# Aligning the operand tiles of the wide matmuls modulo 512 bytes in a bidirectional GLA and RWKV-7 block

## The chip, the core and the metric

The kernel runs on one core of one Trainium2 chip. The metric is device time: microseconds (us) of one execution, as the median of several. A profile of one execution shows every instruction of the five engines: PE (TensorE, whose weight loads are listed apart as PEld), DVE (VectorE), ACT (ScalarE), POOL (GpSimd) and SP, which issues the DMAs.

## What is computed

One encoder block on 2048 tokens of width 1024, in float32:

```
h  = RMSNorm(x)
p  = h @ W_in                              # columns: GLA | RWKV-7 | merge gates
yA = GLA branch, forward + backward        # chunked gated linear attention
yB = RWKV-7 branch, forward + backward     # delta-rule scans
x  = x + (sigmoid(gA) * yA + sigmoid(gB) * yB) @ W_out
u  = conv3(RMSNorm(x) @ ffn_up)            # 2 x 2752 columns, depthwise conv of width 3
x  = x + (silu(u_gate) * u_val) @ ffn_down
out = RMSNorm(x)
```

## The kernel before

**Wide matmuls.** Each float32 operand of a large product is split into a high part (a cast to float32r) and a low part (the rest), and a product is three passes: high by high, high by low, low by high. A matmul loads a stationary tile of 128 x 128 (a weight load, PEld) and streams a moving tile of 128 x 512 past it into one PSUM bank. Nearly all weights pass through two pairs of buffers, `whi` and `wlo`, in the pool `wp`; a tile of a float32 buffer is 512 bytes per partition for a stationary slice and 2048 for a moving one, so every slice of a buffer begins at the same remainder modulo 512 bytes as the buffer does.

**Stages, in order of time.** To 150 us: first norm, transposes, and the value product (`wvh`, `wvl` moving against `hhi`, `hlo`), all in `mm3` (L240). To 1050: the input projection, 116 units of 24 matmuls (L240, `in_tile`: `whi`/`wlo` stationary, `hhi`/`hlo` moving), with the GLA branch and the operands of RWKV-7 woven in as a side thread; it begins with 64 matmuls of the low-rank gate (L402), whose stationary slice has 64 columns. To about 1970: the RWKV-7 chunk recurrence, 32 steps in an order written out by hand, in which a generator `fill` (L1204) places 8 groups of 4 wide matmuls per step between the dependent small ones; these 1248 matmuls are left-over gate tiles and the GLA output projection. To 2100: the RWKV-7 output projection and merge (384 matmuls at L240). To 2310: output projection (768 matmuls at L240, `woh`/`wol` moving against `whi`/`wlo`) and second norm. To 3170: the up projection in two sweeps over 21 pairs of feature tiles (L1494), seven products of 12 matmuls a pair. Two of the seven, with B11 and B21, take `whi`/`wlo` as stationary; five take `s1` to `s4` from the pool `fw`, made by POOL and DVE one pair ahead. The odd 43rd tile adds 96 matmuls with `whi`/`wlo`. To the end: the down projection, 2016 matmuls (L1705 to L1707, `whi`/`wlo` stationary, `wdh`/`wdl` moving), 64 more at L1709 and L1710, and the last norm.

**What sets places and order.** Pools are stacks: left-side pools grow from the low end of SBUF, one after another, and right-side ones (`wp`, `ev`, `op_`, `opx`) from the high end, so a tile's address follows from the sizes of what was opened before it. `const` (the identity `ident`, the table `vec`, `eps_ln`) is the first left pool and stays open to the end. Outside the recurrence a scheduler orders the instructions; a tile on an address that another tile held waits for that tile's last user.

Of the kernel before, what the change touches and what calls it, by code (L numbers as in the profile page):

```python
# [8 lines left out]
F32 = mybir.dt.float32  # L9
# [3 lines left out]
BF16 = mybir.dt.bfloat16  # L13
# [8 lines left out]
T = 2048  # L22
# [144 lines left out]
def _body(tc, A, out, dump=None, upto=99):  # L167
    nc = tc.nc
    L = _vec_layout()
    sync = nc.sync  # L170
    base = ExitStack()

    def pool(stack, name, bufs=1, space=None, **kw):
        if space is None:
            return stack.enter_context(tc.tile_pool(name=name, bufs=bufs, **kw))
        return stack.enter_context(tc.tile_pool(name=name, bufs=bufs, space=space, **kw))
# [22 lines left out]
    d_act = scratch("d_act", [NAT, 128, T])  # L199
    d_mat = scratch("d_mat", [8, 128, 4, BT])  # L200

    const = pool(base, "const")

    def cload(name, shape, dt=F32, key=None):
        t = const.tile(shape, dt, name=name)
# [8 lines left out]
        o = L[name][0] + i  # L214
        return vec[rows, o:o + 1]

    eps_ln = const.tile([128, 1], F32, name="eps_ln")
    nc.gpsimd.memset(eps_ln, 1e-30)

    s_wp = ExitStack()  # L220
    wp = pool(s_wp, "wp", side="right")
    ev = pool(s_wp, "ev", bufs=3, side="right")
# [52 lines left out]
            nc.vector.tensor_tensor(out=ol, in0=pt, in1=oh.bitcast(F32), op=ALU.subtract)  # L275

    FB, MB = (3, 2, 1), 34
# [1 line left out]
    class Halves:  # L279
        def __init__(self, tiles):  # L280
            self.t = tiles
# [7 lines left out]
    s_hb = ExitStack()  # L289
# [4 lines left out]
    s_h = ExitStack()  # L294
# [12 lines left out]
    s_pg = ExitStack()  # L307
# [80 lines left out]
                sync.dma_start(out=dst[:, b * BT:(b + 1) * BT], in_=o)  # L388
            yield

    # GLA low-rank gate inputs: rows = [hi(32) | lo(32)]
    raw = wp.tile([128, 1024], F32, name="wraw", tag="wraw", bufs=1)
    rv = raw[:, 0:256].rearrange("p (a b) -> p a b", a=8)
    sync.dma_start(out=rv, in_=A["waf"])
# [9 lines left out]
        nc.scalar.copy(out=o[0:64, :], in_=ps[0:64, :])  # L404
        sync.dma_start(out=d_af[:, b * BT:(b + 1) * BT], in_=o[0:64, :])

# [1 line left out]
    s1 = ExitStack()  # L408
    s2 = ExitStack()
    gp = pool(s1, "gp", reuse_waits="tile")  # L410
# [5 lines left out]
    nc.gpsimd.memset(g4[64:128, :, 127:128], 0.0)  # L416
    glow = gp.tile([128, 128], U32, name="glow")
    sync.dma_start(out=glow, in_=A["c_glow"])
    gdiag = gp.tile([128, 128], F32, name="gdiag")
    sync.dma_start(out=gdiag, in_=A["c_gdiag"])  # L420
    wa2 = gp.tile([64, 4, 128], F32, name="wa2")
    sync.dma_start(out=wa2, in_=A["wa2"])
    dec = gp.tile([128, 4, 16], F32, name="dec")
# [222 lines left out]
        pl = nc.scalar.preload_act_table_set(LNEXP)  # L646
    act_tail = [pl]

# [1 line left out]
    R = {}  # L650

    def rwkv_open():
# [69 lines left out]
    def rwkv_prep(p, b):  # L722
# [26 lines left out]
            last = nc.scalar.preload_act_table_set(LNEXP)  # L749
        act_tail[0] = last  # L750
        yield
        # normalised key direction
        tmp = R["rp"].tile([128, 512], F32, name="tmp", tag="tmp")
        kk = R["rp"].tile([128, 512], F32, name="kkt", tag="kkt")
        nc.scalar.activation(out=tmp, in_=sk, func=AF.Square, scale=vc("kk", p))
# [54 lines left out]
    def prep():  # L810
        while done[0] < 10:
            yield
        for b in range(NB):
            act_tail[0] = rwkv_shared(b)
            yield
        for p in range(4):
            while done[0] < 13 + 3 * p:
                yield
            for b in range(NB):
                yield from rwkv_prep(p, b)  # L820
# [10 lines left out]
    if upto < 3:  # L831
        return finish(locals())

# [1 line left out]
    s3 = ExitStack()  # L835
    cp = pool(s3, "cp", reuse_waits="tile")
    cl = pool(s3, "cl", reuse_waits="tile")
# [498 lines left out]
    if upto < 4:  # L1336
        return finish(locals())

# [1 line left out]
    s5 = ExitStack()  # L1340
    op_ = pool(s5, "op", side="right", reuse_waits="tile")
    woh = op_.tile([128, KT, D], F32R, name="woh")
# [3 lines left out]
    s_pg = ExitStack()  # L1346
    pg = pool(s_pg, "pg2", bufs=3, space=PSUM)
    s4 = ExitStack()
# [57 lines left out]
    if upto < 5:  # L1406
        return finish(locals())

# [1 line left out]
    s_h2 = ExitStack()  # L1410
    h2a = pool(s_h2, "h2a", reuse_waits="tile")
    h2p = pool(s_h2, "h2p", reuse_waits="tile")
# [7 lines left out]
    s_t = ExitStack()  # L1420
    s_pg = ExitStack()
# [97 lines left out]
    s_pg.close()  # L1519
    s5.close()  # L1520

# [1 line left out]
    # u = W^T h2 by Winograd's form of the 2 x 2 block product: feature tiles (gate, value) x halves of k x blocks of tokens  # L1523
    h2q = pool(s_h2, "h2q", reuse_waits="tile")
    mat(h2q, "T4")
    s6 = ExitStack()
# [49 lines left out]
        nbank[0] += 1  # L1576
        return pus[(nbank[0] - 1) % 8 >= 3].tile([128, 512], F32, name="pu", tag="pu")

    # columns of u: sweep 0 [2 unused | block 1 | block 2], sweep 1 [0 | block 0 | 2 of block 1 | 2 of block 2 | block 3 | 0]
    COLS = ((slice(2, 514), slice(514, 1026)), (slice(1, 513), slice(517, 1029)))  # L1580
    SEG = (((3, 511, 513), (514, 511, 1024)), ((1, 513, 0), (516, 513, 1535)))

# [91 lines left out]
    if upto < 7:  # L1674
        return finish(locals())

# [1 line left out]
    s7 = ExitStack()  # L1678
    fd = pool(s7, "fd", reuse_waits="tile")
    wd0 = pool(s7, "wd0", reuse_waits="tile")  # L1680
    wda = pool(s7, "wda", reuse_waits="tile")
    pd = pool(s7, "pd", space=PSUM)
# [109 lines left out]
def finish(l):  # L1792
    if l["dump"] is not None:
        for n, o in l["dump"].items():
            l["nc"].sync.dma_start(out=o, in_=l[n][0:o.shape[0]])
    for n in ("s5", "s4", "s3", "s_hb", "s_t", "s_pg", "s_h2", "s_h", "s_wp", "base"):
        if n in l:
            l[n].close()

# [18 lines left out]
```

## Time and profile before

| what | value |
|---|---|
| median of 3 executions | 3684.48 us (3683.09 to 3687.15) |
| span of the profiled execution, first to last instruction | 3676.5 us |
| PE busy, matmuls | 3428.3 us (93%) x21208 |
| PE busy, weight loads | 2685.7 us (73%) |
| DVE, ACT, POOL busy | 2402.8 (65%), 1478.6 (40%), 1301.9 us (35%) |
| mean granted TensorE clock | 0.958 |

The profiled execution's span is 8.0 us under the median; the difference lies ahead of the first instruction and behind the last. Matmuls are pipelined: the next one starts while the last one drains, so what a stream of them costs is read from the distance of their starts and not from the busy time of one.

### The profile page before, as it was taken

The numbers are of one execution on the slowest core, as the hardware profiler recorded it, in microseconds if no ns is written. First come the engines' busy times: TensorE is split into PE (matmuls) and PEld (weight loads), VectorE is DVE, ScalarE is ACT, GpSimd is POOL, SyncE is SP. The second block draws the span as 40 slices with busy tenths as digits, with TensorE's granted clock in tenths as the row PEclk, the third lists the DMA queues.
The fourth block names the chain that finished last, engine by engine and source line by source line (L and its number), as shares of the span: only waits on it lengthen the run. The fifth ranks groups of instructions, "written<-read, shape, count | busy, mean of one in ns | idle before, by whom it ended". The sixth has DMA issues, their size and how long they took to land.

```text
span 3676.5 us, 56674 instructions
## 1 busy us (share of the span) xinstructions
PE 3428.3 (93%) x21208; PEld 2685.7 (73%) x21208; DVE 2402.8 (65%) x3926; ACT 1478.6 (40%) x2678; POOL 1301.9 (35%) x1105
## 2 busy tenths in 40 slices
PE   7999999999979899888887899999989999999999
PEld 6787778766667677766665788877768777777777
DVE  5207764687846766766788476889898989723222
ACT  4214443555544444454545333434344344411111
POOL 1122221234442343333325411666676666100000
PEclk9999999999988889998898999999989999999999
DMA  4233444688882655566789846322232222523221
GB/s 152 85 115 108 135 133 134 197 219 230 229 252 92 186 171 163 163 196 184 222 237 307 312 149 192 119 80 78 78 129 91 79 81 81 172 76 113 82 80 62
DMA packets 408338, 547.98 MB, mean 149 GB/s; under 512 B 62528, under 2 KB 251584, under 8 KB 408064
## 3 DMA queue, kind: packets, MB, share of 16 engines
q1 hardware_dynamic: 408064, 544.36, 48.3%
q8 instruction: 167, 2.74, 0.3%
q14 instruction: 107, 0.88, 0.1%
HBM read 361.79 MB, written 181.93 MB: 148 GB/s over the span
## 4 chain that ended last, share of the span: by engine, by line
PE 53%; DVE 21%; DMA 9%; issue 8%; ACT 4%; POOL 3%; SPq 1%; DVEq 0%; ACTq 0%; POOLq 0%
PE pg L240 20%; PE pu L1494 6%; PE pd L1705 4%; PE pd L1706 4%; PE pd L1707 4%; PE pf L1204 4%; DVE cv L1599 2%; DVE tm L915 2%; DVE XX L916 2%; DVE cv L1600 2%; DVE ug L1499 1%; DVE uv L1499 1%; DVE s1l L226 1%; PE psc L867 1%; DMA wraw<-win 1%
## 5 line engine op out<-in xcount | busy, mean ns | idle before, releaser
L876 POOL TENSOR_TENSOR Lt<-Lt,mk 64x512 f32<-64x512 f32 x128 | 148.9, 1163 | 471.4 <-ACT Lt L875 462.5
L1554 POOL TENSOR_TENSOR rw<-rw 128x512 f32<-128x512 f32 x168 | 274.6, 1654 | 4.4 <-DMA rw<-wup 1.0
L1705 PE MATMUL pd<-wdh,whi 128*128 128x512 f32 x672 | 265.4, 397 | 0.9 <-DVE ug L1499 0.9
L1706 PE MATMUL pd<-wdl,whi 128*128 128x512 f32 x672 | 265.2, 395 | 0.0
L1707 PE MATMUL pd<-wdh,wlo 128*128 128x512 f32 x672 | 263.1, 395 | 0.0
L240 PE MATMUL pg<-hhi,whi 128*128 128x512 f32 x928 | 253.5, 408 | 3.7 <-ACT whi L225 3.7
L240 PE MATMUL pg<-hlo,whi 128*128 128x512 f32 x928 | 256.4, 409 | 0.0
L240 PE MATMUL pg<-hhi,wlo 128*128 128x512 f32 x928 | 251.9, 406 | 0.0
L226 POOL TENSOR_TENSOR wlo<-wraw,whi 128x1024 fp32r<-128x1024 f32 x46 | 115.3, 2506 | 349.6 <-PE pg L240 171.8
L240 PEld LDWEIGHTS pg<-hhi,whi 128*128 128x128 f32 x928 | 176.7, 193 | 58.4 <-issue 14.8
L240 PEld LDWEIGHTS pg<-hlo,whi 128*128 128x128 f32 x928 | 176.1, 193 | 56.5 <-issue 18.2
L240 PEld LDWEIGHTS pg<-hhi,wlo 128*128 128x128 f32 x928 | 176.6, 193 | 53.8 <-issue 14.7
L1204 PE MATMUL pf<-fop,whi 128*128 128x512 f32 x576 | 178.6, 446 | 20.3 <-ACT whi L225 13.1
L1598 ACT ACTIVATE cv<-ug,vec 128x511 f32<-128x511 f32 (+1 forms) x88 | 72.1, 819 | 248.7 <-DVE ug L1499 248.7
L225 ACT CAST whi<-wraw 128x1024 fp32r<-128x1024 f32 x114 | 119.7, 1050 | 116.9 <-PE pg L240 52.2
L1204 PEld LDWEIGHTS pf<-fop,whi 128*128 128x128 f32 x576 | 113.4, 208 | 51.7 <-ACT whi L225 15.9
L1705 PEld LDWEIGHTS pd<-wdh,whi 128*128 128x128 f32 x672 | 126.4, 188 | 33.6 <-issue 4.3
L1599 DVE SCALAR_TENSOR_TENSOR cv<-ug,vec,cv 128x511 f32<-128x511 f32 (+1 forms) x88 | 125.3, 1424 | 36.0 <-ACT cv L1598 36.0
L1707 PEld LDWEIGHTS pd<-wdh,wlo 128*128 128x128 f32 x672 | 126.4, 188 | 29.9
L1706 PEld LDWEIGHTS pd<-wdl,whi 128*128 128x128 f32 x672 | 126.5, 188 | 29.4
L1694 ACT CAST whi<-wraw 128x1024 fp32r<-128x1024 f32 (+1 forms) x36 | 35.3, 981 | 275.4 <-PE pd L1706 193.1
L1697 DVE TENSOR_TENSOR wlo<-wraw,whi 128x1024 fp32r<-128x1024 f32 (+1 forms) x36 | 39.3, 1092 | 157.9 <-ACT whi L1694 157.9
(469 smaller groups left out, 8645.9 us busy)
## 6 DMA issues: line engine op xcount, KB each, us to landing
rw<-wup SPq DMA_DIRECT2D x84, 512.0 KB, 3.4
wraw<-win SPq DMA_DIRECT2D x74, 512.0 KB, 4.1
Lt<-d_lt SPq DMA_DIRECT2D x64, 512.0 KB, 6.1
d_lt<-arbk SPq DMA_DIRECT2D x96, 256.0 KB, 3.9
d_gate<-ev SPq DMA_DIRECT2D x64, 256.0 KB, 4.0
X<-d_vt SPq DMA_DIRECT2D x64, 256.0 KB, 4.5
U<-d_vt SPq DMA_DIRECT2D x64, 256.0 KB, 7.5
bj<-d_lt SPq DMA_DIRECT2D x128, 128.0 KB, 4.0
```

Of the source, the lines that this page charges most:

```text
L225: (hi_eng or nc.scalar.copy)(out=hi, in_=src)
L226: (lo_eng or nc.vector).tensor_tensor(out=lo, in0=src, in1=hi.bitcast(F32), op=ALU.subtract)
L240: nc.tensor.matmul(ps, (wh, wh, wl)[ph], (xh, xl, xh)[ph], start=(ph == 0 and i == 0), stop=(ph == 2 and i == n - 1))
L876: nc.gpsimd.tensor_tensor(out=Lt[rk_, e], in0=Lt[rk_, e], in1=mb_[rk_], op=ALU.mult)
L915: nc.vector.tensor_tensor(out=o, in0=X[:, 0:j, j:j + 1].to_broadcast([128, j, w]), in1=X[:, j:j + 1, j + 1:32].to_broadcast([128, j, w]), ...
L1204: nc.tensor.matmul(ps, (wh, wh, wl)[ph][:, k0 + k, :], (hi, lo, hi)[ph][:, k, :], start=i == first[u] and k == 0, stop=i == last[u] and k ...
L1494: nc.tensor.matmul(ps, w_, x_, start=i == 0, stop=i == len(mm) - 1)
L1554: ps_ = lambda o, x, y, op: nc.gpsimd.tensor_tensor(out=o, in0=x, in1=y, op=op)
L1599: nc.vector.scalar_tensor_tensor(out=c, in0=u[:, c0 - 1:c0 - 1 + n], scalar=vc("cw0", m), in1=c, op0=ALU.mult, op1=ALU.add)
L1705: nc.tensor.matmul(ps, a, wdh[k][:, cs], start=(k == 0), stop=False)
L1706: nc.tensor.matmul(ps, a, wdl[k][:, cs], start=False, stop=False)
L1707: nc.tensor.matmul(ps, l, wdh[k][:, cs], start=False, stop=False)
```

## The change

It moves tiles to other addresses. Five edits do it:

- `eps_ln` takes 97 columns where one is used. All left pools behind `const` move up by 384 bytes.
- `gdiag` (ones, with twos on the diagonal) becomes bfloat16: it is loaded into a buffer of `ev`, cast by DVE, and takes 256 bytes less, which shifts the rest of the pool `gp`.
- `const` gets a stack of its own, which is closed ahead of the down projection. The pools of that stage then begin where `const` began.
- A tile `fpad` of 24 columns, which nobody reads, stands first in the pool `fd`.
- Comments are removed, so lines of the new file lie up to five lower or higher.

```diff
-    const = pool(base, "const")
+    s_const = ExitStack()
+    const = pool(s_const, "const")
...
-    eps_ln = const.tile([128, 1], F32, name="eps_ln")
+    eps_ln = const.tile([128, 97], F32, name="eps_ln")[:, 0:1]
...
-    gdiag = gp.tile([128, 128], F32, name="gdiag")
-    sync.dma_start(out=gdiag, in_=A["c_gdiag"])
+    gdiag = gp.tile([128, 128], BF16, name="gdiag")
+    gdf = ev.tile([128, 512], F32, name="ev", tag="ev")[:, 0:128]
+    sync.dma_start(out=gdf, in_=A["c_gdiag"])
+    nc.vector.tensor_copy(out=gdiag, in_=gdf)
...
+    s_const.close()
     s7 = ExitStack()
     fd = pool(s7, "fd", reuse_waits="tile")
+    fd.tile([128, 24], F32, name="fpad")
```

In the two built programs the tiles of the wide matmuls begin at these remainders modulo 512 bytes (moving tile, stationary tile, and their difference):

| matmuls | count | before | after |
|---|---|---|---|
| input projection, L240 | 2784 | 96, 480: 128 | 480, 480: 0 |
| low-rank gate, L402 | 64 | 96, 480: 128 | 480, 480: 0 |
| fill of the recurrence, L1204 | 1248 | 96, 480: 128 | 480, 480: 0 |
| merge, L240 | 384 | 96, 480: 128 | 480, 480: 0 |
| up projection with `whi`/`wlo`, L1494 | 1104 | 96, 480: 128 | 480, 480: 0 |
| down projection, L1705 to L1710 | 2080 | 352, 480: 384 | 480, 480: 0 |
| value product, L240 | 384 | 96, 96: 0 | 480, 480: 0 |
| output projection, L240 | 768 | 480, 480: 0 | 480, 480: 0 |
| up projection with `s1` to `s4`, L1494 | 2520 | 96, 96: 0 | 480, 480: 0 |
| gate product of RWKV-7, L708 | 48 | 384, 96: 288 | 256, 480: 288 |

The small float32 matmuls keep their differences, but for transposes against `ident`, which stays at 128.

The order of the instructions on PE, ACT and POOL is the same in both programs, and so is DVE's but for the added cast. SP issues two loads at another place. At the start of the GLA branch (`wa_1301` and `wa_1303` are the tile `wa2`), SP before:

```order
L418 DMA glow<-c_glow 128x128
L420 DMA gdiag<-c_gdiag 128x128
L330 DMA d_vg<-ev 128x512
L405 DMA d_af<-ev 64x512
L422 DMA wa_1301<-wa 64x512
L480 DMA v<-d_vg 128x4x128
L473 DMA af<-d_af 64x512
L405 DMA d_af<-ev 64x512 x3
L230 DMA wraw<-win 128x1024
```

The same place on SP now:

```order
L419 DMA glow<-c_glow 128x128
L425 DMA wa_1303<-wa 64x512
L331 DMA d_vg<-ev 128x512
L406 DMA d_af<-ev 64x512
L483 DMA v<-d_vg 128x4x128
L476 DMA af<-d_af 64x512
L406 DMA d_af<-ev 64x512 x2
L422 DMA ev<-c_gdiag 128x128
L406 DMA d_af<-ev 64x512
L231 DMA wraw<-win 128x1024
```

The load of `gdiag` has moved behind two stores of `d_af`, since its `ev` buffer was the source of one of them. On SP at the passage from the up to the down projection, before:

```order
L1688 DMA wraw<-wdn 128x1024
L1609 DMA d_act<-cv 128x513 x2
L1756 DMA gf<-gn 128x1024
L1688 DMA wraw<-wdn 128x1024
L1753 DMA ev<-d_act 128x512
```

And the load of `gf` (the gain of the last norm) now:

```order
L1618 DMA cv<-cv 64x513
L1621 DMA d_act<-cv 64x513
L1622 DMA d_act<-cv 64x513
L1618 DMA cv<-cv 64x513
L1761 DMA gf<-gn 128x1024
L1758 DMA ev<-d_act 128x512
```

`gf` now lies on the addresses of `ident` and `vec`; its load has moved behind the last convolution, the last reader of `vec`, and ahead of a load of activations.

## Rows read from the trace of the kernel before

**Rows 1.** Busy us of PE, PEld, DVE, ACT, POOL by stretch; PEclk, DMA, GB/s.

```profile
150.00:732.00 582.00, 576.34 (x2776) 450.81 (x2774) 290.19 (x662) 218.63 (x464) 143.94 (x107) 0.99 0.42 134
732.00:1050.00 318.00, 290.58 (x1072) 200.50 (x1073) 258.47 (x332) 179.78 (x270) 136.65 (x98) 0.92 0.84 222
1050.00:1600.00 550.00, 482.19 (x5719) 379.71 (x5719) 348.31 (x561) 259.52 (x564) 205.92 (x213) 0.90 0.57 169
1600.00:2100.00 500.00, 420.81 (x4469) 326.92 (x4468) 352.54 (x607) 236.02 (x489) 204.80 (x184) 0.89 0.82 253
2310.00:2720.00 410.00, 397.73 (x1714) 320.59 (x1713) 372.30 (x383) 166.42 (x227) 284.33 (x208) 1.00 0.24 83
2800.00:3170.00 370.00, 361.68 (x1557) 291.00 (x1555) 334.00 (x359) 154.69 (x208) 220.25 (x208) 1.00 0.25 86
3170.00:3677.00 507.00, 496.91 (x2082) 390.12 (x2080) 161.33 (x368) 91.54 (x144) 0.00 (x0) 0.99 0.30 95
```

**Rows 2.** The same view, L240 alone (PE, PEld), first two stretches.

```profile
150.00:732.00 582.00, 463.06 (x1886) 351.26 (x1884) 0.99 0.42 134
732.00:1050.00 318.00, 229.44 (x832) 163.77 (x833) 0.92 0.84 222
```

**Rows 3.** The chain by line, in the first six of those stretches.

```profile
by line: PE pg L240 68.4%; PE paf L525 2.8%; PE z L488 2.7%; PE po L564 2.6%; PE po L565 2.5%; PE pkv L541 2.3%; PE pn L708 1.7%; PE pkt L527 1.6%; PE pot L583 1.6%; DMA twal<-d_twal 1.3%; PE pab L526 1.1%; DMA pl<-d_rw 1.0%; PE pw L738 1.0
by line: PE pg L240 16.6%; issue 8.9%; DMA d_lt<-arbk 8.6%; DMA wraw<-win 6.3%; DMA twal<-d_twal 5.9%; PE pw L738 4.7%; DVE arbk L785 4.6%; DMA pl<-d_rw 3.0%; DVE sr L690 2.7%; SPq L788 2.4%; DVE cx L771 2.1%; SPq L808 2.0%; POOL arbk L784 
by line: PE pf L1204 17.3%; DVE XX L916 9.0%; DVE tm L915 8.8%; PE psc L867 6.0%; issue 5.6%; DVE TT L927 4.4%; DVE Q L874 4.1%; DMA wraw<-win 3.9%; DVE wlo L226 3.6%; PE py L1016 3.1%; PE py L1018 2.8%; DMA ev<-d_h 2.6%; DVE X L1009 2.3%; 
by line: PE pf L1204 11.0%; issue 6.3%; DMA gt<-d_gate 5.9%; DMA d_m<-ev 4.6%; PE pg L240 4.3%; DMA ev<-d_gate 3.3%; DVE tm L915 3.2%; DVE XX L916 3.0%; DMA Lt<-d_y 2.8%; PE py L1016 2.5%; PE py L1018 2.4%; DVE TT L927 2.2%; PE psc L867 1.7
by line: PE pu L1494 40.7%; issue 20.1%; DVE cv L1599 8.2%; POOL rw L1554 7.6%; DVE ug L1499 3.6%; DVE uv L1499 3.6%; POOL s3l L226 3.4%; ACT cv L1598 3.2%; POOL halo L1594 2.4%; DVE cv L1600 1.5%; DVE s1l L226 1.4%; DVE cv L1608 1.0%; POOL
by line: issue 22.6%; DVE cv L1600 11.4%; DVE s1l L226 10.4%; DVE ug L1499 9.7%; DVE uv L1499 9.1%; DVE cv L1608 8.1%; ACT cv L1598 7.2%; DVE cv L1599 6.9%; PE pu L1494 6.5%; DVE s4l L226 4.5%; POOL s3l L226 2.3%; ACT s3h L225 0.8%; DVE wdl
```

**Rows 4.** Longest pieces of that chain, output projection: start us, us, what.

```profile
2219.17 14.30 PE pg L240 x63
2242.71 14.30 PE pg L240 x63
```

**Rows 5.** The chain's longest piece in the input projection.

```profile
149.91 131.53 PE pg L240 x566
```

**Rows 6.** PE by time, up projection: start, us, work [idle before <-releaser].

```profile
2461.00 1.07 PE L1494 MATMUL pu<-mT1h,s1h 128*128 128x512 f32 x4
...
2463.73 1.10 PE L1494 MATMUL pu<-mB21h,whi 128*128 128x512 f32 x4
...
2466.52 1.09 PE L1494 MATMUL pu<-mT4h,s3h 128*128 128x512 f32 x4
...
2480.26 1.21 PE L1494 MATMUL pu<-mT3h,s3l 128*128 128x512 f32 x4 [0.74 <-POOL s3l L226]
```

**Rows 7.** PE in order of time, down projection; 53 matmuls left out.

```profile
3329.88 0.39 PE L1705 MATMUL pd<-wdh,whi 128*128 128x512 f32 x1
...
3342.43 0.40 PE L1705 MATMUL pd<-wdh,whi 128*128 128x512 f32 x1
```

**Rows 8.** PE in order of time at the gate product of L708.

```profile
646.50 1.55 PE L708 MATMUL pn<-gh,g 128*128 128x512 f32 x6
647.89 0.86 PE L240 MATMUL pg<-hhi,wlo 128*128 128x512 f32 x3
```

**Rows 9.** PE in order of time, chunk recurrence.

```profile
1622.63 1.20 PE L1204 MATMUL pf<-fop,wlo 128*128 128x512 f32 x4 [2.31 <-DVE wlo L226]
...
1641.12 2.07 PE L1204 MATMUL pf<-fop,wlo 128*128 128x512 f32 x4
```

**Rows 10.** Group of L531: busy us, mean ns | idle before, what ended it.

```profile
L531 POOL TENSOR_TENSOR comb<-comb,gdiag 128x512 f32<-128x512 f32 x16 | 22.4, 1402 | 24.0 <-DVE comb L530 19.8 <-DVE gnr L249 2.6 <-DVE gnt L251 1.0
```

More of the change, by code (lines that the diff above doesn't have):

```diff
@@ L1795, in finish @@
             l["nc"].sync.dma_start(out=o, in_=l[n][0:o.shape[0]])
-    for n in ("s5", "s4", "s3", "s_hb", "s_t", "s_pg", "s_h2", "s_h", "s_wp", "base"):
+    for n in ("s5", "s4", "s3", "s_hb", "s_t", "s_pg", "s_h2", "s_h", "s_wp", "s_const", "base"):
         if n in l:
```

## The prediction

> **What bounds the kernel now.** I read first the busy times by stretch, where a row is a stretch from:to, its length, and then the busy microseconds of PE, PEld, DVE, ACT and POOL [rows 1]. The reader is to see how much of each stretch PE leaves free: 6 of 582 us in the first part of the input projection, 10 of 507 in the down projection, but 27 of 318, 68 of 550 and 79 of 500 between 732 and 2100, and 12 of 410 and 8 of 370 in the two sweeps of the up projection, where DVE is busy for 91% (372 of 410) and 90% (334 of 370). Then the chain of waits by line, one row for each of the first six stretches [rows 3]: to 732 us it runs through L240 for 68.4% and through other PE lines for nearly all the rest; after that PE's wide matmuls hold 16.6%, 17.3%, and 11.0% plus 4.3%, and the rest is small PE work, DVE, and DMA; in the first sweep of the up projection they hold 40.7%, in the second 6.5%.
>
> Last I read what one wide matmul costs, as the distance of starts, since busy times overlap. In the output projection, where moving and stationary tile begin at the same remainder modulo 512 bytes, 63 matmuls take 14.30 us: **227.0 ns** each [rows 4]. In the input projection, where the remainders differ by 128, 566 in an unbroken piece take 131.53 us: **232.4 ns** [rows 5]. In the down projection, with a difference of 384, the starts of two matmuls that are 54 apart lie 12.55 us apart: 232.4 ns [rows 7]. The up projection has both kinds side by side within one pair: 12 matmuls with `s1` (difference 0) from 2461.00 to 2463.73 take 227.5 ns each, the next 12 with `whi` and `wlo` (difference 128) from 2463.73 to 2466.52 take 232.5 [rows 6]. So I take 5.4 ns as the price of an unequal pair of remainders, and 5.0 in the up projection.
>
> Is it the remainder, and not something else that goes with it? Nearly every unequal wide pair has a partner in `wp` at the high end of SBUF. But the output projection takes the same `whi` against `woh`, and is fast; and the RWKV-7 gate product at L708, whose operands both lie in one pool with a difference of 288, is slow: 6 matmuls from 646.50 to 647.89, 231.7 ns each [rows 8]. Neither the stage nor the distance sorts these four cases; the difference of remainders does.
>
> **The change part by part.** It makes the difference 0 for 7,664 wide matmuls; the order on PE, ACT and POOL stays. At 5.4 ns (5.0 for the 1104 of the up projection) all of them are worth 41 us, if each stood on the path at the full clock. Stage by stage:
>
> - Input projection to 732 us: 1886 matmuls [rows 2] x 5.4 ns = 10.2 us. PE is busy for 99% of the stretch and holds the chain, so all of it counts. About 40 of L240 and the 64 narrower ones of L402 before 150 us add 0.3.
> - Input projection from 732 to 1050 us: 832 matmuls [rows 2], 4.5 us at most. The chain gives L240 16.6% of 318 us = 53 us, 227 matmuls: 1.2 us. The rest hides behind DMAs and DVE, which were late anyway.
> - Fill of the recurrence: 1248 matmuls. The chain gives them 17.3% of 550 and 11.0% of 500 us = 150 us, some 645 matmuls, 3.5 us; with a granted clock of 0.90 and 0.89 [rows 1] a fifth of this time runs at the lower level, where no row shows the price, so I count 0.8 of it: 2.8 us. Bounds: 0 (the next step waits for DVE, as at 1622.63 for 2.31 us [rows 9]) and 5.7.
> - Merge: 384 matmuls, 2.1 us at most; the chain's 4.3% of 500 us is 92 matmuls: 0.5 us.
> - Up projection, first sweep: once a pair PE waits for POOL's split of `s3l` (0.74 us at 2480.26 [rows 6]). POOL reaches that split behind work that waits for the last product of the pair before, so the loop runs from the wait through S1, A12, A22 and S4 to POOL and back. The 12 matmuls with A12 lie in it, the 12 with A11 beside it: they only lengthen the wait. 20 pairs x 12 x 5.0 = 1.2 us (bounds 0 and 2.4).
> - Second sweep: the chain leaves PE 6.5% of 370 us, 24 us, about 105 matmuls, of which two in seven are of the changed kind: 0.15 us (bounds 0 and 2.4). DVE and ACT set this loop. The odd tile and the passage between the sweeps add 0.4.
> - Down projection: 2016 x 5.4 = 10.9 us. PE is busy for 497 of 507 us, POOL for none and DVE for a third [rows 1]; I count 98%: 10.7.
>
> Sum: 10.2 + 0.3 + 1.2 + 2.8 + 0.5 + 1.2 + 0.55 + 10.7 = 27.4 us. With all upper ends it is 39, with input and down projection alone 21.
>
> What it adds: one cast on DVE, for which the first GLA gate waits, and a DMA behind two stores of SP; DVE is busy for half of that stretch (290 of 582 us) and PE has projection matmuls to go on with, so I cost it at 0; if that cover were gone, a DMA and a cast would cost a few microseconds once. POOL's 16 products with `gdiag` (1402 ns each [rows 10]) read a bfloat16 operand now; even half as long again would be 11 us on an engine that is busy for a quarter of the stretch. `gf`, the gain of the last norm, is loaded later, yet long before its first use behind all of the first four row tiles, and its wait is for a convolution that SP's next entries need as well: 0. Whether ACT, DVE or POOL mind the shift of their tiles by 384 bytes no row shows; they touch tiles at remainders of every kind now, and I count nothing.
>
> **A rule against it.** The traces show 227.0 against 232.4 ns [rows 4, 5]. The Trainium skill, SBUF — State Buffer, Who interferes with whom, gives PE two independent read ports, one for the moving operand and one for weight loads, and says that PE and ACT never wait on anyone; TensorE: Matmul & The Clock Gate, Step-by-step: what each phase is for, adds that a weight load takes no read bandwidth from the running matmul. By that rule the place of the two tiles could not matter, the sum would be 0 and the time 3684; the rows of this kernel speak against it, so it stays a rival with a small chance.
>
> **The rivals.** (a) *Everything passes through.* If the idle time between 732 and 3170 us shrinks with PE, since small PE work on the chain starts earlier too, the gain nears 39 us: 3646. For it: PE is in order, and each fill matmul stands ahead of a dependent one. Against it: the waits for DVE, POOL and DMAs in [rows 3, 6, 9]. (b) *Less passes.* Input and down projection alone at the 5.0 ns of the up projection, with something of it lost in the waits behind the first: 19 us, or down to 15: 3667. (c) *The remainder is not the cause*, and the slow pairs stay at 232 ns: 3684. Against it are the four cases above; for it, that no row shows a partner in `wp` against a low pool with equal remainders. (d) *Slower, by the clock.* In the recurrence PE waits for DVE (2.31 us at 1622.63), and some 20 us later the same four matmuls are busy for 2.07 instead of 1.20 us [rows 9]: the clock has gone to its lower level, 1.2 instead of 2.4 GHz. The granted 0.90 and 0.89 mean that some 215 of 1050 us run there. If shorter fill makes PE wait longer, more time may. A microsecond at the lower level costs at most half a microsecond, so the loss passes the gain and 0.2% (7.4 us) from 70 us of it on, when the mean clock of the recurrence falls from 0.895 to 0.86; at 0.85 it would give about 3704. Against it: the fill of a step, 32 matmuls, shrinks by only 0.17 us.
>
> **How the numbers follow.** The profiled span is 3676.5 us, the median 3684.5; the 8.0 us outside the span do not change. Forecast: 3684.5 - 27.4 = **3657 us** (gain 22 to 33 us), chance 0.52. (a) 0.17, (b) 0.18, (c) 0.08, (d) 0.05. A measurement of this kernel can tell about 0.2% (7.4 us) from no change. Faster by more than that: forecast, (a) and (b), 0.87; within it: (c), 0.08; slower: 0.05. For 8 times in 10 the range takes in (a) and most of (b): **3643 to 3669 us**; its lower end is (a) with a little less time at the lower clock.
>
> **What would show it.** In the changed kernel's profile: streams of L240, L1204 and the down projection at 227 ns from start to start, as the output projection has now, with L708 still at 232; the down projection's stretch shorter by about 11 us and the input projection's first part by 10; more idle time of PE ahead of `s3l` in the first sweep, by about 0.06 us a pair; a second sweep of the same length; the recurrence shorter by 2 to 4 us at the same granted clock. It would be wrong if the streams stay at 232 ns (then the remainder is not the cause), if they fall and the stretches don't (then PE was not the bound there), or if the granted clock between 732 and 2100 us moves by more than 0.02.

## The result, and the profile after

The changed kernel takes **3661.02 us** (median, 3651.24 to 3662.31) against 3683.78 us for the kernel before on the same chip: ratio 0.9931, 95% interval 0.9914 to 0.9947. On another chip it took 3661.65 against 3678.61 us, ratio 0.9951 (0.9936 to 0.9965). The gain is 17 to 25 us. The forecast was 3657 us, in a range of 3643 to 3669; the time fell inside it, in its upper half.

The busy times by stretch of the changed kernel (columns as in [rows 1]; its down projection begins some 6 us earlier, so the last stretch is shifted):

```profile
150.00:732.00 582.00, 576.75 (x2804) 456.41 (x2803) 293.35 (x671) 221.19 (x469) 141.63 (x107) 0.99 0.42 136
732.00:1050.00 318.00, 285.33 (x1086) 199.70 (x1084) 258.57 (x328) 178.81 (x269) 143.50 (x103) 0.95 0.81 225
1050.00:1600.00 550.00, 479.90 (x5787) 380.60 (x5788) 348.25 (x560) 262.00 (x573) 198.70 (x209) 0.90 0.57 169
1600.00:2100.00 500.00, 421.73 (x4394) 328.20 (x4392) 352.53 (x607) 232.48 (x482) 205.20 (x184) 0.87 0.81 250
2310.00:2720.00 410.00, 392.02 (x1691) 315.43 (x1689) 371.59 (x384) 166.96 (x227) 283.66 (x208) 1.00 0.24 83
2800.00:3170.00 370.00, 358.47 (x1559) 291.04 (x1558) 333.57 (x359) 153.06 (x206) 216.33 (x207) 1.00 0.26 87
3163.00:3658.00 495.00, 485.00 (x2084) 389.42 (x2082) 161.81 (x369) 91.46 (x144) 0.00 (x0) 0.99 0.31 99
```

PE is as full as before in the first and the last stretch, and the down projection now fits into 495 us instead of 507. In the first sweep of the up projection PE is busy for 392.02 us instead of 397.73, with DVE unchanged. Part of that is the window alone: the changed kernel is 8 us ahead here, and 23 matmuls fewer fall into the stretch. What a pair takes is read below.

PE in order of time, changed kernel: the input projection in an unbroken stream and behind small matmuls, the gate product whose difference stayed at 288, one pair of the up projection, the down projection.

```profile
149.99 1.98 PE L241 MATMUL pg<-hlo,whi 128*128 128x512 f32 x8
...
179.00 1.98 PE L241 MATMUL pg<-hhi,wlo 128*128 128x512 f32 x8
...
307.12 2.01 PE L241 MATMUL pg<-hlo,whi 128*128 128x512 f32 x8
308.98 1.98 PE L241 MATMUL pg<-hhi,wlo 128*128 128x512 f32 x8
310.79 1.98 PE L241 MATMUL pg<-hhi,whi 128*128 128x512 f32 x8
312.60 1.07 PE L241 MATMUL pg<-hlo,whi 128*128 128x512 f32 x4
...
643.00 1.56 PE L711 MATMUL pn<-gh,g 128*128 128x512 f32 x6
644.40 0.85 PE L241 MATMUL pg<-hhi,wlo 128*128 128x512 f32 x3
...
2474.36 1.20 PE L1497 MATMUL pu<-mT3h,s3l 128*128 128x512 f32 x4 [0.84 <-POOL s3l L227]
...
3317.07 0.39 PE L1710 MATMUL pd<-wdh,whi 128*128 128x512 f32 x1
...
3329.31 0.39 PE L1710 MATMUL pd<-wdh,whi 128*128 128x512 f32 x1
```

- From 149.99 to 179.00 us 128 matmuls start: 226.6 ns each, where [rows 5] show 232.4. In the down projection 54 matmuls take 12.24 us, 226.7 ns; [rows 7] show 232.4.
- The gate product (L708 before, L711 now) kept its difference and its price: 1.40 us for 6, 233.3 ns, beside 231.7 in [rows 8].
- At 307.12, one matmul behind the small ones of the GLA branch, eight take 1.86 us, 232.5 ns each; the next two groups of eight take 1.81, 226.3 each. Over all streams of L241 up to 732 us, the second to fourth distance behind an interruption is 232 to 233 ns in the mean, the fifth to tenth 228 to 231, and from the eleventh on 226.7. **Behind an interruption a stream needs about ten matmuls before equal remainders pay in full.** The prediction did not have this.
- PE waits 0.84 us for `s3l`, 0.74 before [rows 6]: about the 0.12 us that PE saved in the pair (24 matmuls at 5 ns).

One profile scatters by several microseconds, above all with the time that PE runs at its lower clock. So the next table takes the starts of the same matmuls in all profiles of either layout (five of before, up to nine of the changed layout, those left out that alter the stage itself), as mean and extremes; "low" is the mean time at the 1.2 GHz level by the record of the granted clock, and "turn" the passage between the two sweeps.

| stage | before, us | low | changed, us | low | change | forecast |
|---|---|---|---|---|---|---|
| to 150 | 151.6 (150.2-153.7) | 2.0 | 151.2 (150.0-152.2) | 1.9 | -0.3 | -0.3 |
| 150 to 732 | 582.2 (579.3-584.1) | 8.2 | 574.9 (572.0-578.3) | 7.6 | **-7.3** | -10.2 |
| 732 to 1050 | 316.0 (314.0-317.8) | 45.1 | 313.1 (308.2-317.0) | 39.1 | -2.8 | -1.2 |
| recurrence, to 1975 | 929.5 (924.5-931.9) | 207.4 | 931.1 (927.6-934.7) | 215.0 | **+1.6** | -2.8 |
| merge, output projection, to 2310 | 335.8 | 25.3 | 335.5 | 26.9 | -0.3 | -0.5 |
| up, sweep 1, to 2721 | 412.1 (410.8-413.2) | 0.3 | 413.1 (411.6-413.7) | 0.2 | **+1.0** | -1.2 |
| turn, to 2800 | 79.7 | 25.3 | 78.6 | 21.4 | -1.0 | -0.4 |
| up, sweep 2, to 3171 | 371.0 (370.9-371.1) | 0.0 | 370.1 (369.2-371.1) | 0.0 | -0.9 | -0.15 |
| down, to its end | 493.9 (493.7-494.3) | 0.0 | 481.5 (481.5-481.6) | 0.0 | **-12.3** | -10.7 |

The sum is -22.4 us, where 27.4 was forecast. The first two profiles by themselves differ by 18.6 us (3676.5 and 3657.9): the execution profiled before was a quick one, with the shortest recurrence (924.5 us) of the five.

### The profile page after: what moved, and what is told of

It is laid out like the page before. It is cut to its first block, busy times and chain, and to the rows that moved or that the text cites. A ratio compares the mean times of both kernels' runs of the same rounds, so it can differ in the third digit from the quotient of the medians.

```text
span 3657.9 us, 56677 instructions
## 1 busy us (share of the span) xinstructions
PE 3397.7 (93%) x21208; PEld 2684.3 (73%) x21208; DVE 2404.8 (66%) x3927; ACT 1474.8 (40%) x2678; POOL 1299.4 (36%) x1105
## 4 chain that ended last, share of the span: by engine, by line
PE 33%; DVE 21%; DMA 8%; issue 7%; ACT 4%; POOL 2%; SPq 1%; DVEq 0%; ACTq 0%; POOLq 0%
PE pg L241 6%; PE pd L1710 4%; PE pu L1497 4%; PE pd L1712 4%; PE pd L1711 4%; PE pf L1207 4%; DVE cv L1602 3%; DVE ug L1502 2%; DVE s1l L227 2%; DVE uv L1502 2%; DVE tm L918 2%; DVE TT L930 1%; DVE XX L919 1%; DVE cv L1603 1%; POOL s3l L227 1%
## 5 line engine op out<-in xcount | busy, mean ns | idle before, releaser
L1710 PE MATMUL pd<-wdh,whi 128*128 128x512 f32 x672 | 261.6, 391 | 1.3 <-DVE ug L1502 1.3
L241 PE MATMUL pg<-hhi,whi 128*128 128x512 f32 x928 | 250.2, 404 | 3.6 <-ACT whi L226 3.6
L241 PE MATMUL pg<-hlo,whi 128*128 128x512 f32 x928 | 251.5, 403 | 0.0
L241 PE MATMUL pg<-hhi,wlo 128*128 128x512 f32 x928 | 248.9, 403 | 0.0
L241 PEld LDWEIGHTS pg<-hhi,whi 128*128 128x128 f32 x928 | 176.6, 193 | 55.8 <-issue 15.2
L241 PEld LDWEIGHTS pg<-hhi,wlo 128*128 128x128 f32 x928 | 176.6, 193 | 50.6 <-issue 14.2
L241 PEld LDWEIGHTS pg<-hlo,whi 128*128 128x128 f32 x928 | 174.8, 191 | 51.8 <-issue 16.6
L1602 DVE SCALAR_TENSOR_TENSOR cv<-ug,vec,cv 128x511 f32<-128x511 f32 (+1 forms) x88 | 125.4, 1425 | 36.9 <-ACT cv L1601 36.9
L1710 PEld LDWEIGHTS pd<-wdh,whi 128*128 128x128 f32 x672 | 126.1, 188 | 30.2 <-issue 4.6
```

The source lines that it names most:

```text
L241: nc.tensor.matmul(ps, (wh, wh, wl)[ph], (xh, xl, xh)[ph], start=(ph == 0 and i == 0), stop=(ph == 2 and i == n - 1))
L1602: nc.vector.scalar_tensor_tensor(out=c, in0=u[:, c0 - 1:c0 - 1 + n], scalar=vc("cw0", m), in1=c, op0=ALU.mult, op1=ALU.add)
L1710: nc.tensor.matmul(ps, a, wdh[k][:, cs], start=(k == 0), stop=False)
```

## The experiments

**1. Down projection alone, and everything but it.** The first kernel puts the down projection back to a difference of 384 bytes and leaves the rest aligned:

```
-    fd.tile([128, 24], F32, name="fpad")
+    fd.tile([128, 120], F32, name="fpad")
```

> The changed kernel with one size altered: the unused tile ahead of the down projection is 480 bytes long instead of 96, so its moving tiles begin 384 bytes off again, as before, and all other wide matmuls stay equal. If the difference of remainders is the cause: the down projection's matmuls stand 232.4 ns apart again, its stretch is 11 to 12 us longer than in the changed kernel, and the time is about 3672 (12 us under the kernel before). If closing the constants' pool or the later load of the last norm's gain brought the down projection's gain: it stays at 227 ns, and the time at 3661.

The second is the kernel before with the last block of the diff alone (constants released ahead of the down projection, `fpad` of 24 columns).

> The kernel before with the down projection's part of the change alone (constants closed ahead of it, unused tile of 96 bytes): equal remainders in the down projection, the old ones everywhere else. If the difference is the cause and each stage stands for itself: 227 ns in the down projection, 232.4 in the input projection, a gain of 11 to 12 us: about 3672. If the place of the stationary buffers at the high end of SBUF mattered as such: 232 ns stays, 3684. If the two halves of the change overlap (a gain given back): more than 12 us here.

Measured: 0.9983 (0.9973 to 0.9994) for the first, about 6 us (2 to 10) under the kernel before, where 12 had been expected: what lies ahead of the down projection gave about half as much as was thought. For the second 0.9973 (0.9963 to 0.9983), about 10 us (6 to 14), where 11 to 12 had been expected. PE in order of time in the first, 54 matmuls in 12.54 us, 232.2 ns:

```profile
3325.01 0.39 PE L1710 MATMUL pd<-wdh,whi 128*128 128x512 f32 x1
...
3337.55 0.40 PE L1710 MATMUL pd<-wdh,whi 128*128 128x512 f32 x1
```

And in the second, 54 matmuls in 12.24 us, 226.7 ns:

```profile
3330.42 0.39 PE L1708 MATMUL pd<-wdh,whi 128*128 128x512 f32 x1
...
3342.66 0.39 PE L1708 MATMUL pd<-wdh,whi 128*128 128x512 f32 x1
```

So the stage's gain goes and comes with 24 or 120 columns of an unused tile, and with nothing else. The product of the two ratios is 0.9956. The whole change gave 0.9951 (0.9936 to 0.9965) on another chip, which agrees; the first measurement, 0.9931 (0.9914 to 0.9947), lies lower.

> The changed kernel itself, unaltered, beside the kernel before on this chip, as the measure for the part experiments. If the parts add up (0.9983 for everything but the down projection, 0.9973 for the down projection alone), the ratio is about 0.9956 or lower; the first measurement gave 0.9931. Theory that the low-clock pieces scatter by some 4 us from one profile to the next: the down stage is again shorter by 11 to 12 us, the piece from 150 to 700 us by 7 to 10 us, and the difference at the start of the up projection lies anywhere between -5 and -11 us. Rival (the layout itself lengthens the low-clock time): the extra low-clock piece of 3.4 us in the first 50 us and the one near 480 us come again at the same places.

The down projection was again 12.2 us shorter (493.7 to 481.5), the stretch from 150 to 700 us 5.4, less than the 7 to 10 expected. The difference at 2310 us was only -0.3, so the bounds of -5 to -11 set for it were too narrow: this profile ran 17 us more at the lower clock up to there than the one of before. The rival is not borne out. The low-clock piece of the first 50 us did not come again, and three of the five profiles of the layout before have one there. The only other piece before 700 us, at 419 us in the changed kernel's first profile, came again at 417, but one profile of the layout before has a piece at 424 too.

**2. Which differences cost.** Unused tiles between the weight tiles of the down projection give each group of three feature tiles a difference of its own; the second kernel has other differences, and three of the first at other places in the loop.

```
+    WPAD = {3: 8, 6: 8, 9: 16, 12: 32, 15: 48, 18: 8}
     def load_wd(q, k, raw):
+        if k in WPAD:
+            q.tile([128, WPAD[k]], F32, name=f"wpad{k}")
```

> The changed kernel with unused tiles between the weights of the down projection, so that three or four k in a row begin at 0, 32, 64, 128, 256, 448 and 480 bytes behind the stationary tile's remainder. If any unequal pair costs the same: 227 ns apart at 0 and 232 to 233 at each of the others, the down projection about 9 us longer. If the cost grows with the distance: a staircase from 227 at 32 to 233 at 256, and 448 and 480 like 64 and 32. If only some part of the remainder counts (modulo 64, 128 or 256): the steps that are multiples of it stay at 227. If two independent ports serve the operands: 227 at all seven.

> The changed kernel with unused tiles between the weight tiles of the down projection, so that k = 0-2, 3-5, 6-8, 9-11, 12-14, 15-17, 18-21 lie at differences of 256, 288, 320, 352, 416, 0 and 64 bytes: other differences, and those seen before (256, 0, 64) at other places in the loop over k. Theory that the difference itself sets the spacing: 256 and 0 at 227 to 228 ns, 64 at 229, as in the first sweep of differences, and the others anywhere between 228 and 234. Rival (the place in the loop over k sets it, or what lies beside it): k = 0-2 stays fast whatever its difference, 15-17 stays at 233, and 12-14 at 228.

PE in order of time: the first matmul of a group of 18, in the first kernel (differences 32, 64, 128, 256, then 448 begins) and in the second (288, 320, 352, 416, 0, then 64 begins).

```profile
3327.82 0.40 PE L1714 MATMUL pd<-wdh,whi 128*128 128x512 f32 x1
...
3332.02 0.39 PE L1714 MATMUL pd<-wdh,whi 128*128 128x512 f32 x1
...
3336.14 0.39 PE L1714 MATMUL pd<-wdh,whi 128*128 128x512 f32 x1
...
3340.31 0.40 PE L1714 MATMUL pd<-wdh,whi 128*128 128x512 f32 x1
...
3344.44 0.39 PE L1714 MATMUL pd<-wdh,whi 128*128 128x512 f32 x1
```

```profile
3321.26 0.40 PE L1714 MATMUL pd<-wdh,whi 128*128 128x512 f32 x1
...
3325.46 0.39 PE L1714 MATMUL pd<-wdh,whi 128*128 128x512 f32 x1
...
3329.58 0.40 PE L1714 MATMUL pd<-wdh,whi 128*128 128x512 f32 x1
...
3333.79 0.39 PE L1714 MATMUL pd<-wdh,whi 128*128 128x512 f32 x1
...
3337.99 0.39 PE L1714 MATMUL pd<-wdh,whi 128*128 128x512 f32 x1
...
3342.10 0.40 PE L1714 MATMUL pd<-wdh,whi 128*128 128x512 f32 x1
```

A group that takes 4.20 us has 233.3 ns a matmul, one of 4.12 has 228.9. Over all row tiles, from the seventh matmul of a group on, the mean distance of starts is (384 from the kernel before):

| difference, bytes | 0 | 32 | 64 | 128 | 256 | 288 | 320 | 352 | 384 | 416 | 448 | 480 |
|---|---|---|---|---|---|---|---|---|---|---|---|---|
| ns | 226.8 | 233.3 | 228.9 | 231.9 | 228.0 | 233.3 | 228.9 | 233.3 | 232.7 | 233.9 | 233.3 | 233.3 |

The same place in the loop has 228.0 ns with 256 and 233.9 with 416, another 233.3 with 448 and 226.7 with 0: the place is not it, the difference is. But it is not "any difference": 256 costs 1 ns, 64 and 320 cost 2, the others 5 to 7. Values 256 apart behave alike (32 and 288; 64 and 320; 128 and 384), so what counts is nearly the remainder modulo 256, and 64 is better than 448 (64 the other way), so the sign matters. In this table the stationary tile always begins at 480. That other places with the same difference behave alike is shown for 0 (96 and 96 in the up projection before, 480 and 480 here: about 227) and, in six matmuls each, for 288 (L708 before, L711 now); for the rest it is not shown.

**3. The fill of the recurrence.** In the changed kernel the groups of the fill are made longer.

```
-    FW, F2, F3, F4 = 2, 2, 2, 2
+    FW, F2, F3, F4 = 4, 0, 4, 0
```

> The changed kernel, but the fill of a recurrence step is set out as 4, 0, 4, 0 units (groups of 16 matmuls) instead of 2, 2, 2, 2 (groups of 8). Theory that a stream needs some eight matmuls behind small ones before it runs at 227 ns: the mean spacing of the fill matmuls falls from 230.5 to about 229, since half of them now stand at the ninth place or later, and the first eight stay at 230 to 233. Rival (the fill matmuls are slowed all along by the DVE and ACT traffic of the recurrence): the mean stays at 230.5 and the later places are no faster. The time of the whole is not forecast by either: two gaps of the recurrence are left without fill and PE may wait there, so it may well be slower by a few us.

The mean distance of starts in the fill at the full clock was 232.6 ns before, 230.5 in the changed kernel, and 229.2 here. By place in a group, the second to fourth matmul took 233 ns in the changed kernel, the fifth to eighth 230, those from the tenth on 227 to 229; here the same places took 231 to 234, 228 to 230, and 228 to 229. The settling is confirmed; the later places are a little slower than in unbroken streams. The kernel as a whole is 2.0% slower (ratio 1.0200, 1.0178 to 1.0221), where a few us had been expected. The same stretch of time, 1050 to 1975 us, in one profile of the kernel before, in the changed kernel, and here:

```profile
1050.00:1975.00 925.00, 795.41 (x9721) 623.38 (x9719) 617.54 (x1036) 435.25 (x951) 331.28 (x344) 0.89 0.65 191
```

```profile
1050.00:1975.00 925.00, 788.88 (x9711) 619.68 (x9711) 627.13 (x1056) 441.14 (x964) 331.96 (x342) 0.88 0.66 193
```

```profile
1050.00:1975.00 925.00, 744.57 (x8963) 598.03 (x8964) 564.80 (x928) 402.21 (x869) 297.39 (x311) 0.83 0.57 167
```

Where two of four gaps are left without fill, PE waits (its busy time falls from 788.88 to 744.57) and the granted clock falls from 0.88 to 0.83; the recurrence takes 1015.3 instead of 931.1 us, 338 of them at the lower level instead of 215. That is rival (d)'s mechanism at full size, brought on here by gaps without fill and not by shorter fill.

**4. What sets the up projection.** The multiply of the GLU is left out on both layouts, about 1.4 us of DVE in a pair (the value alone is stored, so these two kernels compute less).

```
-            nc.vector.tensor_tensor(out=v, in0=v, in1=g, op=ALU.mult)
```

> The kernel before without the GLU multiply on VectorE (value times silu of gate; the value alone is stored), about 1.4 us of VectorE time a pair. Theory that VectorE with its hand-offs from ACT sets the first sweep's period (20.29 us a pair): the period falls to PE's own sum, 60 matmuls at 227.5 and 24 at 232.5 = 19.2 us, or a little above. Rival, as the prediction had it (the loop from PE to POOL's split of s3l and back): the period stays within 0.2 us of 20.29.

> The changed kernel without the same GLU multiply. Theory: with VectorE relieved PE holds the pair, and the equal remainders now show: the period is 0.10 to 0.14 us below that of the kernel before without the multiply (24 matmuls at 5 ns), some 4 to 5 us over both sweeps. Rival (PE and POOL loop): period about 20.22 us, 0.06 below the other. If both periods are equal, the up projection is bound by something else again.

The chain of waits in the first sweep (start us, us, what), layout before and changed layout:

```profile
2439.95 200.18 PE pu L1494 x873
```

```profile
2439.95 136.69 PE pu L1497 x603
```

The chain is PE alone now, without a wait: 229.3 ns a matmul and 226.7, which for the 84 of a pair is 19.26 and 19.04 us. With the multiply both layouts take 20.28 to 20.29. So DVE, not the loop over POOL, held the pair; relieved of 1.4 us it lets PE through. POOL itself waits for DVE's sum of `uv` once in each pair (changed kernel, POOL in order of time):

```profile
2488.19 1.11 POOL L1597 COPY halo<-uv 128x2 f32<-128x2 f32 x1 [5.07 <-DVE uv L1502]
```

With PE as the bound, the alignment pays 0.22 us a pair. That is twice the 0.12 forecast, because the aligned neighbours gain too: at each change from an unequal group to an equal one the stream has to settle (the equal matmuls took 227.9 ns before and 226.7 now, the others 233.0 and 226.7). But it does not last. In the changed layout 14 pairs of the first sweep and 8 of the second take 19.04 us; then DVE falls behind once more, and a pair takes 19.3 us in the first sweep and 19.4 in the second, which is more than the 19.27 that the layout before keeps to the end. Over both sweeps the two kernels differ by 1.7 us (393.1 and 392.1, 357.8 and 357.1 us, one profile each), where 4 to 5 had been expected.

**5. Giving POOL more, and less.** DVE's split of `s4l` moved to POOL:

```
-        w["S4"] = parts(fw, ("s4h", "s4l"), r1[:, b], nc.vector, 4)
+        w["S4"] = parts(fw, ("s4h", "s4l"), r1[:, b], nc.gpsimd, 4)
```

> The changed kernel with the low part of s4 (128x512, 0.68 us on DVE, one a pair of the up projection) computed by POOL. The changed kernel's period of 20.28 us a pair is the same as before although 24 of its 84 matmuls are 5 ns shorter. If DVE with its two hand-offs to ACT sets that period: it falls by up to 0.6 us a pair, 42 pairs, some 25 us: about 3636. If POOL's chain to the s3 split sets it (where PE is seen to wait): POOL gets 1.3 us more in front of or behind that split, and the period stays or grows by up to 1.3 us: 3661 to 3716.

Ratio 0.9978 (0.9969 to 0.9986), 10 us or more slower than the changed kernel (0.9951 and 0.9931): 20.18 us a pair in the first sweep, 0.1 less than in the changed kernel (up to 0.6 less had been expected if DVE set the pair), and 20.47 instead of 20.09 in the second. The view of lines, DVE in the first sweep, GLU multiply, changed kernel and then this one:

```profile
L1611 DVE TENSOR_TENSOR cv<-cv 128x511 f32<-128x511 f32 x24 | 16.2, 677 | 0.0
```

```profile
L1611 DVE TENSOR_TENSOR cv<-cv 128x511 f32<-128x511 f32 x24 | 29.5, 1227 | 0.0
```

The multiply itself was not touched; its mean is 1227 ns instead of 677, because one of its two in a pair now falls beside POOL's additions and takes 1.78 us. In return one convolution step (L1602 for `ug`) takes 1104 ns instead of 1618, so DVE's sum hardly changes. The changed kernel shows the same by itself (DVE and POOL in order of time):

```profile
2473.41 1.45 DVE L1602 SCALAR_TENSOR_TENSOR cv<-uv,vec,cv 128x511 f32<-128x511 f32 x1 [0.89 <-ACT cv L1601]
...
2477.91 5.21 POOL L1557 TENSOR_TENSOR rw<-rw 128x512 f32<-128x512 f32 x3
2478.48 1.78 DVE L1602 SCALAR_TENSOR_TENSOR cv<-ug,vec,cv 128x511 f32<-128x511 f32 x1
2480.19 1.78 DVE L1602 SCALAR_TENSOR_TENSOR cv<-uv,vec,cv 128x511 f32<-128x511 f32 x1
2481.89 1.78 DVE L1603 SCALAR_TENSOR_TENSOR cv<-ug,vec,cv 128x511 f32<-128x511 f32 x1
...
2484.19 0.74 DVE L1603 SCALAR_TENSOR_TENSOR cv<-uv,vec,cv 128x511 f32<-128x511 f32 x1
```

Three convolution steps inside POOL's additions take 1.78 us; one of the same size at 2484.19, when POOL is idle, takes 0.74. (The 0.89 us ahead of the first row is DVE waiting for ACT, twice in a pair; for the rest of it DVE is back to back.) The Trainium skill, SBUF — State Buffer, Who interferes with whom, says that a DVE instruction with both inputs in SBUF contends with GpSimd's reads over a shared port; these rows agree, at 1.78 against 0.74 us. So POOL is not free capacity for DVE. The opposite was tried last: the small copies to and from `halo` go from POOL to ACT.

```
-            nc.gpsimd.tensor_copy(out=halo[:, m, 0:2], in_=u[:, 2:4])
+            nc.scalar.copy(out=halo[:, m, 0:2], in_=u[:, 2:4])
```

(and likewise the second copy to `halo` and the one from it)

> The changed kernel with the small copies to and from the halo (128 x 2 and 128 x 4 elements) on ACT instead of POOL; the result is the same. In the profile of the changed kernel POOL spends about 2.9 us a pair of the first sweep on them, and two of them stand right ahead of POOL's splits. VectorE's operations on SBUF take 0.74 us alone and 1.78 us beside POOL's additions. Theory that VectorE sets the pair and is stretched by POOL's work: the period of 20.28 us falls, to 19.9 to 20.2 us by a part of the 2.9 us, and PE's equal remainders do the rest once PE is the bound (19.04 us): the kernel is 2 to 16 us faster than the changed kernel, ratio 0.991 to 0.995 against 0.9951 for the changed kernel on this chip. Rival (ACT's copies wait for the last sum of a pair and hold back ACT's splits behind them): the period rises and the kernel is slower than the changed one. If small copies do not slow VectorE, the period stays at 20.2 to 20.3 us and the second sweep is the same within 0.05 us a pair.

3654.14 us, ratio **0.9914** (0.9899 to 0.9929): faster than the kernel before, and than the changed kernel on either chip by the medians (its intervals overlap with the changed kernel's first one). Sweep 1 takes 396.3 instead of 413.1 us; its pairs settle at 19.59 us, below the 19.9 to 20.2 expected, and PE's waits for `s3l` there are nearly gone (0.26 us in a pair). A stretch of the first sweep, changed kernel and then this one (columns as in [rows 1]):

```profile
2440.00:2680.00 240.00, 229.94 (x994) 184.54 (x994) 217.08 (x225) 94.86 (x128) 164.77 (x118) 1.00 0.23 77
```

```profile
2440.00:2680.00 240.00, 237.28 (x1034) 192.94 (x1033) 214.81 (x234) 106.24 (x184) 144.10 (x74) 1.00 0.24 82
```

DVE is nearly as full as before (217.08 and 214.81 of 240 us), so a pair of 20.28 us holds 18.3 us of DVE's work and one of 19.59 holds 17.5: its work shrank by about as much (0.8) as the period (0.7), as the theory has it. That the small copies as such had slowed it is not shown, since POOL's other operations moved too and `s3l` came earlier.

Sweep 2 takes 376.6 instead of 370.1: there DVE's split `s1l` lies beside POOL's split `wlo` for 1.55 us instead of 1.26 (view of lines, second sweep, changed kernel and this one) and takes 0.31 us longer in each pair, which is as much as the loss.

```profile
L227 DVE TENSOR_TENSOR s1l<-rw,s1h 128x1024 fp32r<-128x1024 f32 x15 | 35.2, 2344 | 0.0
```

```profile
L227 DVE TENSOR_TENSOR s1l<-rw,s1h 128x1024 fp32r<-128x1024 f32 x15 | 39.8, 2653 | 0.0
```

The copies on ACT in the first sweep only might keep the 17 us and not lose the 6; that was not tried.

**6. The clock in the recurrence.** Two more profiles of the kernel before:

> The kernel before, unaltered, for its low-clock time in the recurrence (1050 to 1975 us): three profiles of the layout before show 198.9, 205.1 and 213.4 us there, six of the changed layout 209.4 to 222.6. If the layout has no part in it, this look lies anywhere between 199 and 223 us, and the stage takes 824 to 826 us plus half of that. If equal remainders bring more low-clock time, it stays below 213.

> The kernel before once more, for the same: two theories as for the look ahead of it.

They show 212.4 and 207.4 us at the lower level and 931.2 and 931.9 us for the stage (825 and 828 us plus half of that; the second lies 2 us above the expected 824 to 826). The layout before now has 199 to 213 us at the lower level in five profiles, the changed layout 209 to 223 in eight. The ranges overlap and the means differ by 8 us. Whether the layout has a part in it is not settled.

## Why the prediction was right, and where its sum was off

- **The cause** (difference of remainders, 5.4 ns): right. The streams fell to 226.6 to 226.7 ns, L711 with its old difference stayed at 233, and an unused tile of 96 more columns brought 232 back. Rival (c) is out, and with it the rule of the Trainium skill's SBUF — State Buffer, Who interferes with whom, as a forecast here: two independent read ports would make all differences alike, and the runs show 226.8 to 233.9 ns over twelve of them. The reading "equal or not" was too coarse: 256 is nearly as good as 0.
- **Input projection, 10.2 us:** the failed term. It took 1886 matmuls at the price of an unbroken stream, measured on one [rows 5]. From about 300 us on, small matmuls of the GLA branch break the stream every few groups, and what follows them has to settle first. The mean distance fell from 232.5 to 228.25 ns: 4.2 x 1886 = 8.0 us; the stage gained 7.3.
- **732 to 1050, 1.2 us:** 2.8 measured, inside the bounds, but with 6 us less time at the lower clock, which is worth 3 us by itself; nothing can be read from it.
- **Recurrence, 2.8 us:** not there; the stage is 1.6 us longer, with a scatter of 3. The mechanism was mis-sized in the same way as the input projection: fill comes in groups of eight, all of them within the settling, so a matmul gained 2.1 ns and not 5.4 (645 x 2.1 = 1.4 us). With half a microsecond counted off for each at the lower clock the stage is 2.2 us shorter, and the 8 us more at the lower level take that back. This would be rival (d) at small size; that it is more than scatter was not shown, and the cause stays open.
- **Merge and output projection, 0.5 us:** 0.3 measured, less than the scatter.
- **Up projection, first sweep, 1.2 us:** the step fails as argued. PE does wait for POOL's `s3l`, as [rows 6] say, but POOL waits for DVE's last sums, and DVE is back to back but for two waits of 0.89 us for ACT. PE's saving went into the wait (0.74 to 0.84 us), that of the 12 matmuls with A12 as well as that of the 12 with A11; the period stayed at 20.28. The chain's 40.7% for L1494 in [rows 3] misled: a chain that goes back along PE from a wait shows PE's work even where another engine set the date. DVE's 91% in [rows 1] was the better witness, and experiment 4 decides it.
- **Second sweep, turn, 0.55 us:** 1.9 measured; the sweep by itself 0.9, partly from profiles that begin it with a few quick pairs.
- **Down projection, 10.7 us:** 12.3. All of it passes, as said; the price was too low by a tenth, since the mean of all starts before, 232.7 ns, lay above the piece of [rows 7], and the mean after is 226.7: 6.0 x 2016 = 12.1.
- **Side costs at 0:** POOL's products with the bfloat16 `gdiag` take 1276 ns instead of 1402 [rows 10]; no wait for the cast or for `gf` stands out.

```profile
L534 POOL TENSOR_TENSOR comb<-comb,gdiag 128x512 f32<-128x512 f32 x16 | 20.4, 1276 | 23.8 <-DVE comb L533 19.7 <-DVE gnr L250 2.6 <-DVE gnt L252 1.0
```

- **The granted clock**, one of the signs that the prediction set: it rose from 0.92 to 0.95 between 732 and 1050 us and fell from 0.89 to 0.87 between 1600 and 2100. Over 732 to 2100 us as a whole it is 0.90 in both profiles.
- **"8.0 us outside the span"** was wrong, without harm to the result: the profiled executions whose own time is on record show 1.7 to 2.1 us outside (3659.89 against 3657.9 for the changed kernel). By that the execution profiled before took an estimated 3678.5 us; the other 6 were its distance from the median.

That the sum came within 5 us is in part luck: the terms that were too high (input projection 2.9, recurrence 4.4, first sweep 2.2 us, merge 0.2) stand against terms that were too low (732 to 1050 1.6, turn and second sweep 1.35, down projection 1.6).

Rival (a) did not occur; what happened lies between the forecast (a gain of 22 to 33 us) and rival (b) (15 to 19): the gain came from the two stages that PE fills, and the rest gave about 3 us net of gains and losses.

## What to carry to other kernels

Where wide matmuls follow each other without a break, compare the remainders at which moving and stationary tile begin: a few unused columns ahead of a pool were worth 2.5% of the down projection. Count such a gain only in stretches that PE fills, and in full only from about the tenth matmul of an unbroken group on. Where PE is 97% busy but waits a little in each round, look for the engine that is back to back (here DVE), and before moving its work to POOL look at how long its operations take beside POOL's.

## What the runs showed of the hardware that was not expected

- The distance of starts of back-to-back 128 x 512 matmuls depends on the difference of the start remainders, and values 256 bytes apart gave nearly the same (within 1.2 ns, stationary tile at 480): 227 to 228 ns at 0 and 256, 229 at 64 and 320, 232 to 234 at the other values tried; 64 and 448 are not alike (228.9 and 233.3).
- A stream with equal remainders runs at 231 to 234 ns for its first four or so matmuls behind small ones, at 228 to 231 for the next, and reaches 227 at about the tenth. Why, no run here shows.
- Convolution steps of DVE, which read SBUF alone, took 1.78 us beside POOL's additions and 0.74 without; DVE's sums that read PSUM (L1502) took 0.68 us, and at most 0.70, also beside POOL's work.
